# Hybrid encoder layer: two of the output projection's weight chunks split into hi and lo during the in-projection, kept in DRAM, and loaded in the attention

## The chip, the cores and the metric

One NeuronCore of a Trainium2 chip runs the whole program; the other cores are idle. The metric is the device time of one execution in microseconds (us). The kernel before was run three times beside the runs of this study.

## What is computed

One layer of a hybrid encoder in fp32, on 1024 prompt tokens and 256 sample tokens (1280 in all, ten tiles of 128), with model width 1024:

```python
n = _rms_norm(h, g_mix, NORM_EPS)
z = jnp.einsum('bsd,dc->bsc', n, w_in).astype(f32)
qa, ka, va, qb, kb, vb = jnp.split(z, cuts, axis=-1)
oa = _diff_attention(qa, ka, va, lam, _alibi_slopes())
oa = _rms_norm(oa, g_subln, SUBLN_EPS) * (1.0 - lam_init)
ob = _gqa_attention(qb, kb, vb)
mixed = jnp.concatenate([oa, ob], axis=-1).astype(h.dtype)
h = h + jnp.einsum('bsc,cd->bsd', mixed, w_out)
```

Mixer A is differential attention (4 heads, two softmax maps each), mixer B grouped-query attention (8 query heads, 2 key heads, with rotary positions). The output projection multiplies the 1024 columns of `mixed` by `w_out` (1024 x 1024). A squared-ReLU MLP, a gated per-layer input and a last norm follow; the change does not touch them.

## The kernel before, in words

**Precision.** TensorE multiplies fp32r operands. Where fp32 accuracy is wanted, an operand is split into hi (a rounding copy, mostly by ACT) and lo (the difference, by DVE or POOL), and a product is made of three matmuls: hi x hi, hi x lo, lo x hi.

**Stages.** In the in-projection (to about 200 us) units of matmuls (`psb`, `psa`) go through the tokens; `norm_rope` (L296 to L318) norms and rotates a `psb` tile with ACT (`sq`), DVE (`zg`, `rb`, `ro`) and POOL. The results are split and written to DRAM (`qd`, `kd`, `vad`, `vbd`) and loaded again as `qt`, `kt`, `vt` in the attention. In the attention (200 to about 600 us) each unit computes scores (`sc`, PE), exponentials (`p`, ACT), transposes (`tr`, PE), their split (`ph` by ACT, `pl` by DVE) and the products with the values (`av`, PE). Mixed outputs are split into `ml` and written to DRAM as `md`. Beside the attention runs side work on PE: first the rest of the q and k columns (`qk_rest`, L811), then the output projection (`out_proj`, L887) in two passes over four chunks each of 128 rows of `w_out`: (0, 1, 4, 5), then (2, 3, 6, 7).

**Weights of the output projection.** `opw_dma` (L860 to L872) loads a chunk's raw rows as two halves of 128x512 (256 KB each), into the tails of residual tiles (`h_sb`) or into slot Q1 (`wor`). `opw_split` (L874 to L885) makes hi on ACT (L883) and lo on POOL (L884), each 128x512, in tiles `ow`. In the first pass chunk 0's raw rows come early, from `qk_rest` (L840), into Q1; chunks 1 and 4 go to the tails of `h_sb`; chunk 5 goes to Q1 as soon as chunk 0's split has read it. Chunks 2 and 3, for the second pass, are loaded and split while the first pass runs. `load_mt` (L890 to L898) loads a token tile of `mixed` (`mt`, 512 KB) and with it rows of x (`h_sb<-in_x`, 512 KB) to which the result is added.

**Early work.** `early_w1` (L468 to L503) is a side generator of the in-projection: it loads blocks of the MLP's first weights, combines and splits them and writes them to DRAM (`wed`). `along` (L505) steps it between the units of the in-projection, and `drain(early)` finishes it at the end.

**What sets the order.** The program is written as interleaved generators; a framework then fixes each engine's static order by a simulated timeline. Every DMA of interest is issued by SP in one queue; each issue also waits until the eighth DMA before it has landed, so a late transfer holds the issues behind it.

Of the kernel before, what the change touches and what calls it, by code (L numbers as in the profile page):

```python
# [14 lines left out]
F32 = mybir.dt.float32  # L15
F32R = mybir.dt.float32r
# [24 lines left out]
def f(ap):  # L41
    return ap.bitcast(F32)
# [3 lines left out]
def encoder_kernel(ctx: ExitStack, tc: tile.TileContext, x, xT, pT, w_in, w_out, w_ff1, w_ff2, w_gate, w_proj,  # L46
# [3 lines left out]
    LEAD = {4: 2000., 5: 2000., 6: 2000.}  # L50
    PRE = 14000
    Y = (0, 1, 1)
    XA = 1
    QM = 0
    AW = (-7, -6, -5, -4)
# [409 lines left out]
    NEW = 2  # L465
    wed = {(p, i): dp.tile([P, 2, 4, P], F32, name=f"wed{p}_{i}") for p in range(NEW) for i in range(1, 8)}

    def early_w1():  # L468
        for p in range(NEW):
            raws = [slot(f"Q{kh}", [P, 4, 256], F32, "w1e") for kh in range(2)]  # L470
            for kh, raw in enumerate(raws):
                load(raw, w_ff1[kh * 512:kh * 512 + 512, p * 256:(p + 1) * 256].rearrange("(k p) c -> p k c", p=P))
            a11, a12, a21, a22 = (raws[x][:, :, c * P:c * P + P] for c in range(2) for x in range(2))
            yield
            for kh, raw in enumerate(raws):
                for k in range(4):
                    S.activation(raw[:, k], raw[:, k], AF.Copy, scale=gmlp[:, 4 * kh + k:4 * kh + k + 1])
            yield

            def out(i, src):  # L480
                hl = bp.tile([P, 2, 4, P], F32R, tag="xt", name="w1o", bufs=2)
                S.activation(hl[:, 0], src, AF.Copy)
                V.tensor_tensor(hl[:, 1], src, f(hl[:, 0]), op=ALU.subtract)
                dma(wed[p, i], f(hl[:]))

            out(1, a11)
            t = bp.tile([P, 2, 4, P], F32, tag="qkl", name="w1t", bufs=1)
            s3, s2 = t[:, 0], t[:, 1]
            V.tensor_tensor(s3, a11, a21, op=ALU.subtract)
            V.tensor_tensor(s2, a22, s3, op=ALU.subtract)  # L490
            yield
            for i, src in ((6, s2), (7, s3), (2, a12)):
                out(i, src)
                yield
            V.tensor_tensor(s3, a12, s2, op=ALU.subtract)
            V.tensor_tensor(s2, a21, a22, op=ALU.add)
            for i, src in ((5, s2), (4, a22), (3, s3)):
                out(i, src)
                yield

    def along(main, side, skip, every):

# [311 lines left out]
    def qk_rest():  # L814
        w = qk_split(qk_dma(0))
        for n, (h, col, dst, sc) in enumerate(qk_items):
            more = n + 1 < len(qk_items)
            raws = qk_dma(n + 1) if more else None
            wh, wl = w
            for ci, (c0, cn) in enumerate(TCH):  # L820
                ps = pj("psa")
                pr = []
                for k in range(KD):
                    pr += [(wh[k], xh[:, k, c0:c0 + cn]), (wl[k], xh[:, k, c0:c0 + cn]), (wh[k], xl[:, k, c0:c0 + cn])]
                yield from mm_gen(ps[:, :cn], pr, 3)

                def evac(ps=ps, c0=c0, cn=cn, dst=dst, sc=sc, eng=V if LV and not more and ci == 2 else G):
                    hl = zp.tile([P, 2, 512], F32R, tag="zl", name="zl")
                    z = f(hl[:, 1, :cn])
                    V.scalar_tensor_tensor(z, ps[:, :cn], sc, R[:, c0:c0 + cn], op0=ALU.mult, op1=ALU.mult)  # L830
                    S.activation(hl[:, 0, :cn], z, AF.Copy)
                    eng.tensor_tensor(hl[:, 1, :cn], z, f(hl[:, 0, :cn]), op=ALU.subtract)
                    dma(dst[:, :, c0:c0 + cn].rearrange("v p t -> p v t"), f(hl[:, :, :cn]))

                deferred.append(evac)
                yield 0.0
                if ci == 0 and more:
                    w = qk_split(raws)
                elif ci == 0:
                    op_state["w0"] = opw_dma(0, "Q1")  # L840
            qk_done.append(n)

    op_state = {}
# [27 lines left out]
            dma(raws[i], w_out[ch * P:(ch + 1) * P, i * 512:i * 512 + 512])  # L871
        return raws  # L872

    def opw_split(raws):  # L874
        n = next(ow_n) % 5
        if n < 2:
            w = slot(f"H{5 + n}", [P, 2, D], F32R, "ow")
            a, b = w[:, 0], w[:, 1]
        else:
            a, b = (slot(f"W{2 * n - 4 + i}", [P, D], F32R, "ow")[:] for i in range(2))  # L880
        for i, raw in enumerate(raws):
            c = slice(i * 512, i * 512 + 512)
            S.activation(a[:, c], raw, AF.Copy)  # L883
            G.tensor_tensor(b[:, c], raw, f(a[:, c]), op=ALU.subtract)  # L884
        return a, b  # L885

    def out_proj(chs, ws, ahead, banks, first):  # L887
# [10 lines left out]
                        dma(h_row(t_), x[t_ * P:(t_ + 1) * P])  # L898

        if first:  # L900
            raws = [op_state.pop("w0"), opw_dma(chs[1]), opw_dma(chs[2])]
            for n in range(4):
                for _ in range(Y[n > 0]):
                    yield 0.0
                ws.append(opw_split(raws.pop(0)))
                if n == 0:
                    raws.append(opw_dma(chs[3], "Q1"))
                    load_mt(0)
        else:
            raws = []  # L910
# [774 lines left out]
```

## Time and profile before

| | |
|---|---|
| median of 3 runs | 1704.44 us (1703.85 to 1705.3) |
| the profiled execution's own time | 1704.98 us |
| its span, first to last instruction | 1703.2 us |
| granted TensorE clock, mean over the span | 0.997 |
| busy: PE, DVE, ACT, POOL | 98%, 69%, 51%, 39% |
| DMA | 278.28 MB, mean 163 GB/s |

Times in the rows are from the span's start. Busy is the share of a stretch in which the engine executes an instruction; an idle time in square brackets stands before the instruction, with what ended it. The granted clock is 1.00 at 2.4 GHz.

### The profile page before, as it was taken

To read this page: it belongs to the slowest core of one execution; us is meant where nothing else is said; L and a number is where in the kernel's file an instruction comes from. 1 tells how busy PE (TensorE), PEld (TensorE's weight loads), DVE (VectorE), ACT (ScalarE), POOL (GpSimd) and SP (SyncE) were. 2 spreads that over 40 slices of the span, in tenths; PEclk is the share of its full clock that TensorE was granted. 3 is DMA by queue.
4 is the path that set the end of the run, shared out by engine and by line. 5 is a ranking of instruction groups with operands and counts; after the bars stand their busy time and mean duration, and the time that the engine had idled before them with its cause. 6 is when DMAs were issued, how large, how long until landed. Compare 5 with 4: busy or idle time off the path is not lost.

```text
span 1703.2 us, 27269 instructions
## 1 busy us (share of the span) xinstructions
PE 1666.5 (98%) x9849; PEld 1488.6 (87%) x9849; DVE 1177.2 (69%) x2119; ACT 868.3 (51%) x1749; POOL 658.4 (39%) x647
## 2 busy tenths in 40 slices
PE   8999999999899999999999999999999999999997
PEld 8999889888788888889999999998888888888886
DVE  7788588787887878578666666665655865445666
ACT  8543377677766767674333233333433333354644
POOL 1224455555653445424655666520533400001441
PEclk9999999999999999999999999999999999999999
DMA  9767844433953624495343434359666466532111
GB/s 316 228 225 246 233 141 124 138 92 108 269 156 118 165 69 127 134 308 181 132 156 127 138 131 150 122 198 376 202 216 195 130 205 193 169 114 73 35 44 50
DMA packets 191867, 278.28 MB, mean 163 GB/s; under 512 B 13674, under 2 KB 121076, under 8 KB 191732
## 3 DMA queue, kind: packets, MB, share of 16 engines
q1 hardware_dynamic: 189988, 271.28, 49.7%
q0 software_dynamic: 1600, 5.24, 1.0%
q8 instruction: 78, 1.28, 0.3%
q14 instruction: 57, 0.47, 0.1%
q10 hardware_dynamic: 144, 0.00, 0.0%
HBM read 182.63 MB, written 88.61 MB: 159 GB/s over the span
## 4 chain that ended last, share of the span: by engine, by line
PE 79%; DVE 7%; ACT 4%; issue 4%; DMA 3%; POOL 3%; SPq 0%; POOLq 0%; ACTq 0%; DVEq 0%
PE psa L255 6%; PE sc L642 5%; PE psb L255 5%; PE av L720 5%; PE pso L255 4%; PE tr L696 3%; PE psv L255 3%; PE psg L1576 2%; DVE pl L707 1%; DMA h_sb<-in_x 1%; DVE mm L659 1%; PE f__16295 L156 1%; PE f__15255 L156 1%; PE f__16637 L156 1%; PE f__15600 L156 1%
## 5 line engine op out<-in xcount | busy, mean ns | idle before, releaser
L1373 ACT ACTIVATE ao<-ar 128x1280 fp32r<-128x1280 f32 x56 | 71.3, 1275 | 187.5 <-PE f__16299 L156 37.8
L642 PE MATMUL sc<-kt,qt 128*128 128x512 f32 (+1 forms) x576 | 157.0, 392 | 6.9 <-ACT p L667 4.6
L707 DVE TENSOR_TENSOR pl<-tr,ph 128x512 fp32r<-128x512 f32 x204 | 137.9, 684 | 33.5 <-ACT ph L702 32.3
L1375 DVE TENSOR_TENSOR ao<-ar,ao 128x1280 fp32r<-128x1280 f32 x56 | 93.3, 1666 | 94.0 <-ACT ao L1373 94.0
L702 ACT ACTIVATE ph<-tr 128x512 fp32r<-128x512 f32 x204 | 119.8, 595 | 56.9 <-PE tr L696 50.4
L255 PE MATMUL pso<-ow,mt 128*128 128x512 f32 x480 | 119.4, 395 | 4.2 <-ACT ow L883 1.8
L696 PE MATMUL tr<-ident,p 128*128 128x128 f32 x768 | 116.0, 274 | 5.7 <-DVE pl L707 4.9
L642 PEld LDWEIGHTS sc<-kt,qt 128*128 128x128 f32 x576 | 99.4, 190 | 24.8 <-ACT p L667 6.1
L1576 PE MATMUL psg<-gw,n 128*128 128x512 f32 (+1 forms) x504 | 115.4, 384 | 0.0
L696 PEld LDWEIGHTS tr<-ident,p 128*128 128x128 f32 x768 | 91.8, 141 | 22.5 <-DVE pl L707 8.6
L1576 PEld LDWEIGHTS psg<-gw,n 128*128 128x128 f32 x504 | 90.8, 188 | 19.5
L255 PEld LDWEIGHTS pso<-ow,mt 128*128 128x128 f32 x480 | 87.5, 188 | 22.4 <-DVE osq L747 2.0
L1094 POOL TENSOR_SCALAR w1r<-w1r,gmlp 128x256 f32<-128x256 f32 x112 | 79.7, 728 | 67.6 <-DMA w1r<-in_w_ff 67.6
L720 PE MATMUL av<-ph,vt 128*128 128x256 f32 x544 | 102.4, 289 | 1.1 <-ACT ph L702 0.5
L681 POOL TENSOR_SCALAR p<-p,rl 128x1024 f32<-128x1024 f32 x64 | 76.0, 1188 | 51.3 <-DVE rl L679 46.6
L1167 ACT ACTIVATE w<-w1s 128x512 fp32r<-128x512 f32 x56 | 35.2, 628 | 116.5 <-POOL w1s L1174 49.4
L659 DVE TENSOR_REDUCE mm<-sc 128x1 f32<-128x1024 f32 (+1 forms) x80 | 84.2, 1055 | 8.8 <-PE sc L642 8.3
L720 PE MATMUL av<-pl,vt 128*128 128x256 f32 x408 | 89.5, 301 | 0.0
L720 PEld LDWEIGHTS av<-ph,vt 128*128 128x128 f32 x544 | 82.4, 190 | 6.6 <-ACT ph L702 0.9
L667 ACT ACTIVATE p<-sc,mm 128x1024 f32<-128x1024 f32 x64 | 71.3, 1114 | 25.5 <-DVE mm L659 18.5
L655 DVE CUSTOM_DVE_ANT_0 p<-sc,dist 128x1024 f32<-128x1024 f32 x64 | 77.6, 1218 | 7.9 <-PE sc L642 3.8
L664 ACT ACTIVATE p<-p,mm 128x1024 f32<-128x1024 f32 x64 | 73.5, 1149 | 18.0 <-DVE mm L655 17.3
(1520 smaller groups left out, 4717.2 us busy)
## 6 DMA issues: line engine op xcount, KB each, us to landing
ar<-ad SPq DMA_DIRECT2D x56, 640.0 KB, 4.0
w2r<-in_w_ff SPq DMA_DIRECT2D x56, 512.0 KB, 4.6
qt<-qd SPq DMA_DIRECT2D x160, 128.0 KB, 3.1
ad<-q SPq DMA_DIRECT2D x64, 320.0 KB, 3.0
ad<-qs SPq DMA_DIRECT2D x48, 320.0 KB, 2.2
w1r<-in_w_ff SPq DMA_DIRECT2D x28, 512.0 KB, 4.3
md<-ml SPq DMA_DIRECT2D x40, 256.0 KB, 2.5
mt<-md SPq DMA_DIRECT2D x20, 512.0 KB, 5.4
```

The source lines that it names most:

```text
L255: PE.matmul(ps, a, b, start=i == 0, stop=i == n - 1)
L642: PE.matmul(ps[:, h0:h0 + n], shared["q"][:, cc, v, i * P:(i + 1) * P], kt[:, s0 + h0:s0 + h0 + n], start=v == 0, stop=v == 1)
L655: V.tensor_tensor_reduce(out=p[:, :sn], in0=ps[:, :sn], in1=dst_t[:, off:off + sn], scale=SLOPES[idx], scalar=3.0e38, op0=ALU.add, op1=ALU ...
L659: V.tensor_reduce(out=st["m", i][:, 0:1], in_=ps[:, :sn], axis=AX.X, op=ALU.max, negate=True)
L681: G.tensor_scalar(p[:, :sn], p[:, :sn], rl[:, 0:1], 1.0, op0=ALU.mult, op1=ALU.mult)
L696: PE.transpose(t[:, jj, i * P:(i + 1) * P], st["ws"][i][:, j * P:(j + 1) * P], ident)
L702: S.activation(ph, st["tr", j2], AF.Copy)
L707: V.tensor_tensor(pl, st["tr", j2], f(st["ph", j2][:]), op=ALU.subtract)
L720: PE.matmul(st["av"][:, :256], x_, y_, start=j2 == 0 and n == 0, stop=j2 == nj - 1 and n == len(pr) - 1)
L1094: G.tensor_scalar(raw[:, k], raw[:, k], gmlp[:, 4 * kh + k:4 * kh + k + 1], 1.0, op0=ALU.mult, op1=ALU.mult)
L1375: V.tensor_tensor(ao[:, 1], a, f(ao[:, 0]), op=ALU.subtract)
L1576: ends[:] = [PE.matmul(ps, a, b, start=m == 0, stop=m == len(pr) - 1)]
```

## The change

`early_w1` gets a last loop: for chunks 0 and 1 it loads the raw rows of `w_out` (512 KB), splits them in halves with ACT and DVE, and writes hi and lo to new DRAM tiles `wod` (four writes of 512 KB). In the first pass of the output projection `opw_fetch` loads hi and lo of these chunks from there (two DMAs of 512 KB per chunk) into the `ow` tiles; only chunks 4 and 5 are loaded raw and split, both in the tails of `h_sb`. The load from `qk_rest` and Q1's use for chunk 5 go away. `YF` is not used.

```diff
+    OWP = (0, 1)
+    wod = {ch: dp.tile([P, 2, D], F32, name=f"wod{ch}") for ch in OWP}
+
     def early_w1():
...
+        for ch in OWP:
+            raw = bp.tile([P, 2, 512], F32, tag="qkl", name="wo_r", bufs=1)
+            load(raw, w_out[ch * P:(ch + 1) * P, :].rearrange("p (i c) -> p i c", i=2))
+            yield
+            for i in range(2):
+                hl = bp.tile([P, 2, 512], F32R, tag="xt", name="wo_o", bufs=2)
+                S.activation(hl[:, 0], raw[:, i], AF.Copy)
+                V.tensor_tensor(hl[:, 1], raw[:, i], f(hl[:, 0]), op=ALU.subtract)
+                dma(wod[ch][:, :, i * 512:i * 512 + 512], f(hl[:]))
...
                 if ci == 0 and more:
                     w = qk_split(raws)
-                elif ci == 0:
-                    op_state["w0"] = opw_dma(0, "Q1")
...
-    def opw_split(raws):
+    def opw_slot():
         n = next(ow_n) % 5
         if n < 2:
             w = slot(f"H{5 + n}", [P, 2, D], F32R, "ow")
-            a, b = w[:, 0], w[:, 1]
-        else:
-            a, b = (slot(f"W{2 * n - 4 + i}", [P, D], F32R, "ow")[:] for i in range(2))
+            return w[:, 0], w[:, 1]
+        return tuple(slot(f"W{2 * n - 4 + i}", [P, D], F32R, "ow")[:] for i in range(2))
+
+    def opw_fetch(ch):
+
+        ab = opw_slot()
+        for v in range(2):
+            dma(f(ab[v]), wod[ch][:, v])
+        return ab
+
+    def opw_split(raws):
+        a, b = opw_slot()
         for i, raw in enumerate(raws):
...
         if first:
-            raws = [op_state.pop("w0"), opw_dma(chs[1]), opw_dma(chs[2])]
-            for n in range(4):
-                for _ in range(Y[n > 0]):
-                    yield 0.0
-                ws.append(opw_split(raws.pop(0)))
+            raws = [opw_dma(ch) for ch in chs if ch not in OWP]
+            for n, ch in enumerate(chs):
+                if ch in OWP:
+                    ws.append(opw_fetch(ch))
+                else:
+                    yield 0.0
+                    ws.append(opw_split(raws.pop(0)))
                 if n == 0:
-                    raws.append(opw_dma(chs[3], "Q1"))
                     load_mt(0)
```

**In the in-projection, SP's queue after the change**, from the last writes of the MLP's early weights (`wed`) on; `wo_r` is the raw chunk, `wo_o` its split.

```order
L488 DMA wed_3_1301<-w1o 128x1024
L94 DMA wo_r<-in_w_out 128x1024
L583 DMA qt<-qd_64 64x2x256
L337 DMA qd_66<-qkl 128x2x512
L337 DMA qd_67<-qkl 128x2x512
L567 DMA kt<-kd_68 64x1280 x4
L404 DMA qd_60<-zl 128x2x512
L513 DMA wod_1306<-wo_o 256x1x512 x2
L94 DMA wo_r<-in_w_out 128x1024
L404 DMA qd_60<-zl 128x2x512
L513 DMA wod_1307<-wo_o 256x1x512
L811 DMA rawq<-in_w_in 128x4x128
```

On ACT the first pair of copies stands between the square of one `psb` tile and the split of a `psa` tile (`zl`):

```order
L301 ACTIVATE sq<-psb,rstd_95 128x256
L511 ACTIVATE wo_o<-wo_r 128x512 x2
L402 ACTIVATE zl<-zl 128x512
L140 ACTIVATE rq4u<-rq4v 128x4
L141 ACTIVATE rr<-rq4u 128x4
```

All rows with `wo_r` and `wo_o` are new; the rest stands as before, `zl` right behind `sq`. On DVE the subtractions come behind `ro` and ahead of the next `zg`.

**At the start of the output projection, SP's queue before:**

```order
L871 DMA h_sb<-in_w_out 128x512 x4
L894 DMA mt<-md_79 128x8x128
L898 DMA h_sb<-in_x 128x1024 x2
L894 DMA mt<-md_79 128x8x128
L898 DMA h_sb<-in_x 128x1024
L569 DMA qt<-qd_66 64x2x256
L871 DMA wor<-in_w_out 128x512 x2
L569 DMA qt<-qd_66 64x2x256 x2
L559 DMA vt_6352<-vbd_78 128x10x128
L871 DMA h_sb<-in_w_out 128x512 x4
L594 DMA md_79<-ml 128x2x256
```

and now (`ow<-wod` are the fetches; the first four `h_sb<-in_w_out` are chunks 4 and 5, the later four chunks 2 and 3):

```order
L883 DMA h_sb<-in_w_out 128x512 x4
L897 DMA ow<-wod_1306 128x1024 x2
L915 DMA mt<-md_79 128x8x128
L919 DMA h_sb<-in_x 128x1024 x2
L897 DMA ow<-wod_1307 128x1024 x2
L915 DMA mt<-md_79 128x8x128
L919 DMA h_sb<-in_x 128x1024
L583 DMA qt<-qd_66 64x2x256 x2
L573 DMA vt_6369<-vbd_78 128x10x128
L883 DMA h_sb<-in_w_out 128x512 x4
L608 DMA md_79<-ml 128x2x256
```

The fetches stand ahead of the first `mt` and of the raw rows of chunks 2 and 3; `wor` is gone. (In both, one more pair of `mt` and x rows and a further `qt` stand in rows left out here.) PE's order there before, from the first matmuls of the projection (`pso`) on:

```order
L255 MATMUL pso<-ow,mt 128x512 x4
L720 MATMUL av<-ph,vt_3166 128x256 x2
L696 MATMUL tr<-ident,p 128x128 x4
L720 MATMUL av<-pl,vt_3166 128x256 x2
L642 MATMUL sc<-kt,qt 128x512 x4
L255 MATMUL pso<-ow,mt 128x512 x3
L696 MATMUL tr<-ident,p 128x128 x4
```

and now:

```order
L656 MATMUL sc<-kt,qt 128x512 x4
L256 MATMUL pso<-ow,mt 128x512 x3
L710 MATMUL tr<-ident,p 128x128 x8
L656 MATMUL sc<-kt,qt 128x512 x4
L734 MATMUL av<-ph,vt_4918 128x256 x4
```

The first four `pso` no longer stand ahead of `av`; the projection begins where its second group stood.

**ACT at the copies of chunk 5 and chunk 2 before** (`ow<-wor` and the `ow<-h_sb` behind it):

```order
L664 ACTIVATE p,ll<-p,mm 128x1024 x2
L702 ACTIVATE ph<-tr 128x512
L883 ACTIVATE ow<-wor 128x512 x2
L702 ACTIVATE ph<-tr 128x512
L734 ACTIVATE osq<-av 128x256
L735 ACTIVATE o<-av,gsub 128x256
L702 ACTIVATE ph<-tr 128x512
L745 ACTIVATE or<-av,eps_t 128x256
L883 ACTIVATE ow<-h_sb 128x512
L702 ACTIVATE ph<-tr 128x512
L746 ACTIVATE or<-or 128x256
L664 ACTIVATE p,ll<-p,mm 128x1024
```

and now:

```order
L749 ACTIVATE o<-av,gsub 128x256
L716 ACTIVATE ph<-tr 128x512
L759 ACTIVATE or<-av,eps_t 128x256
L716 ACTIVATE ph<-tr 128x512
L760 ACTIVATE or<-or 128x256
L678 ACTIVATE p,ll<-p,mm 128x1024 x2
L904 ACTIVATE ow<-h_sb 128x512
L716 ACTIVATE ph<-tr 128x512
L681 ACTIVATE p,ll<-sc,mm 128x1024
L904 ACTIVATE ow<-h_sb 128x512
```

The copies of `wor` are gone, and chunk 2's first copy has moved behind both exponentials. Up to the start of the output projection the orders of PE, DVE, ACT and POOL differ only by the new copies and subtractions; from there to about 550 us (of the time before) they are dealt anew.

## Rows read from the trace of the kernel before

**Rows 1.** The page, part 1: busy us, share of the span, instructions.

```profile
PE 1666.5 (98%) x9849; PEld 1488.6 (87%) x9849; DVE 1177.2 (69%) x2119; ACT 868.3 (51%) x1749; POOL 658.4 (39%) x647
```

**Rows 2.** Windows: stretch, length; busy us of each engine; granted clock, DMA share, GB/s.

```profile
426.00:468.00 42.00, 37.28 (x227) 32.02 (x226) 33.98 (x58) 31.88 (x64) 28.17 (x27) 0.96 1.01 269
442.00:446.00 4.00, 2.04 (x12) 1.51 (x11) 3.32 (x6) 3.95 (x9) 4.00 (x3) 1.00 1.04 355
458.00:462.00 4.00, 1.81 (x10) 1.15 (x9) 1.43 (x3) 2.62 (x6) 1.97 (x2) 0.98 1.13 236
462.00:466.00 4.00, 4.00 (x14) 3.29 (x14) 3.33 (x6) 1.80 (x5) 0.91 (x2) 0.60 1.02 312
```

**Rows 3.** Waits of PE in 400:560: total us, times, longest us.

```profile
PE sc L642 <- ACT p L667: 2.4, 3, 1.7
...
PE pso L255 <- ACT ow L883: 1.8, 1, 1.8
```

**Rows 4.** Timeline of PE, 440:476: start us, us, instruction, count, idle before.

```profile
446.76 1.07 PE L255 MATMUL pso<-ow,mt 128*128 128x512 f32 x4
...
448.59 1.09 PE L642 MATMUL sc<-kt,qt 128*128 128x512 f32 x4
449.52 0.86 PE L255 MATMUL pso<-ow,mt 128*128 128x512 f32 x3
...
460.00 0.50 PE L255 MATMUL pso<-ow,mt 128*128 128x512 f32 x1 [1.76 <-ACT ow L883]
...
461.36 0.86 PE L255 MATMUL pso<-ow,mt 128*128 128x512 f32 x2 [0.42 <-POOL ow L884]
...
463.58 1.93 PE L642 MATMUL sc<-kt,qt 128*128 128x512 f32 x4
465.35 2.91 PE L255 MATMUL pso<-ow,mt 128*128 128x512 f32 x12
```

**Rows 5.** Timeline of ACT, 438:476.

```profile
440.14 1.16 ACT L883 ACTIVATE ow<-wor 128x512 fp32r<-128x512 f32 x2
441.73 0.63 ACT L883 ACTIVATE ow<-h_sb 128x512 fp32r<-128x512 f32 x1 [0.43 <-DMA h_sb<-in_w_out]
...
459.32 1.32 ACT L883 ACTIVATE ow<-wor 128x512 fp32r<-128x512 f32 x2 [3.06 <-DMA wor<-in_w_out]
...
464.93 0.63 ACT L883 ACTIVATE ow<-h_sb 128x512 fp32r<-128x512 f32 x1 [1.34 <-DMA h_sb<-in_w_out]
...
467.90 1.14 ACT L664 ACTIVATE p<-p,mm 128x1024 f32<-128x1024 f32 x1
```

**Rows 6.** Timeline of SP's DMA queue, 436:476.

```profile
439.51 0.56 SPq L894 DMA_DIRECT2D mt<-md  x1
```

**Rows 7.** Windows, in-projection.

```profile
175.00:185.00 10.00, 10.00 (x73) 9.29 (x72) 8.22 (x18) 4.63 (x11) 6.26 (x7) 1.00 0.34 116
```

**Rows 8.** Timeline of SP's DMA queue, 150:186.

```profile
162.97 0.54 SPq L484 DMA_DIRECT2D wed<-w1o  x1
```

**Rows 9.** DMA issues in 155:175: count, KB each, median us to landing.

```profile
wed<-w1o SPq DMA_DIRECT2D x3, 512.0 KB, 4.6
kt<-kd SPq DMA_DIRECT2D x4, 320.0 KB, 6.7
...
qd<-zl SPq DMA_DIRECT2D x1, 512.0 KB, 7.9
```

**Rows 10.** Timeline of ACT, 160:186.

```profile
163.80 0.47 ACT L300 ACTIVATE sq<-psb,rstd 128x256 f32<-128x256 f32 x1 [0.82 <-PE psb L255]
166.29 0.63 ACT L401 ACTIVATE zl<-zl 128x512 fp32r<-128x512 f32 x1 [2.02 <-DVE zl L400]
```

**Rows 11.** Timeline of DVE, 160:186.

```profile
161.33 0.69 DVE L483 TENSOR_TENSOR w1o<-w1t,w1o 128x512 fp32r<-128x512 f32 x1 [0.94 <-ACT w1o L482]
...
170.14 0.48 DVE L301 SCALAR_TENSOR_TENSOR zg<-psb,rstd,gq 128x256 f32<-128x256 f32 x1 [0.45 <-ACT sq L300]
```

**Rows 12.** Timeline of PE, 174:180.

```profile
176.09 0.36 PE L255 MATMUL psb<-whp,xh 128*128 128x256 f32 x1
```

More of the change, by code (lines that the diff above doesn't have):

```diff
@@ L52, in encoder_kernel @@
     Y = (0, 1, 1)
+    YF = 2
     XA = 1
```

## The prediction

> **What bounds the kernel now.** I read the page's busy shares first, then the windows around the start of the output projection, then the waits and the engines' timelines there, and last the DMA lists and the in-projection.
>
> TensorE (PE) is busy 98% of the span [rows 1], so only what makes PE idle or slow counts. The windows show one such place: in 458:462 PE is busy for 1.81 of 4 us, and in 462:466 it is busy throughout at a granted clock of 0.60 [rows 2]. The waits name the cause: a matmul of the output projection (`pso`) waits 1.8 us for ScalarE's (ACT's) hi copy of w_out, line 883 [rows 3]. In the timelines, ACT stood 3.06 us in front of the copies of chunk 5 (`wor`) because their data had not landed [rows 5]; PE then stood 1.76 us for ACT and 0.42 us for GpSimd's (POOL's) lo [rows 4]. 1.76 + 0.42 = 2.18 us is all the idle time of 458:462 (4 - 1.81 = 2.19). Slow matmuls follow: four `sc` take 1.93 us at 463.58 against 1.09 at 448.59 [rows 4]. Behind all of it is the DMA queue, whose share is 1.01 at 269 GB/s through 426:468 [rows 2].
>
> **What the change takes away.** Chunk 5 is no longer loaded into Q1 in the middle of this stretch: its raw rows come with the first loads, and chunks 0 and 1 are not split here. So the stall above goes:
> - PE's idle time, 1.76 + 0.42 = 2.2 us;
> - the half clock behind it: 4 us at 0.60 lose 4 x 0.40 = 1.6 us [rows 2]. The two levels are 1.2 and 2.4 GHz, and 0.60 is a mean over both.
>
> Together **-3.8 us**. Of four chunk splits, two leave ACT and POOL here. ACT's pair of copies at 440.14 only filled a wait: ACT stood again, 0.43 us, for the first raw half at 441.73 [rows 5], and that load keeps its place at the head of SyncE's (SP's) queue. So PE's 1.7 us behind the exponential (`sc<-ACT p` [rows 3], of which the windows show 442:446 with PE at 2.04 of 4) stays, and I cost that part at nothing.
>
> **What it adds in the attention.** SP now issues four fetches of 512 KB (2.1 MB) and no `wor` load there (0.52 MB less): 1.57 MB more before the first raw half of chunk 2. The queue is full, so this is time for whatever stands behind. I price it by the rows: at 355 GB/s (442:446) 4.4 us, at 269 (426:468) 5.8, at 236 (458:462) 6.7 [rows 2]. I take 355, because 442:446 moves mostly x rows of 128x1024, the shape of a fetch.
>
> First new wait: `mt` for the first token tile was issued at 439.51 [rows 6] and was there at the latest at 446.76, when PE began `pso` without waiting [rows 4]. Now two fetches, 1.05 MB, stand ahead of it: 3.0 us at 355, so it lands by 449.7 or before. PE's order has lost four `pso` matmuls ahead of that place, so PE comes there 0.93 us before the 449.52 where the second `pso` group stood, at about 448.6. The wait is 0 to 1.1 us at this rate, 2.1 at 269, 2.6 at 236. 446.76 is an upper bound of the old landing, so I take **+0.9**.
>
> Second new wait: ACT's copy of chunk 2's first half. Before, ACT stood 1.34 us for that load, which ended at 464.93 [rows 5], and that hid under slow matmuls. Now the load ends 4.4 us later, 469.3. ACT comes to the copy after both exponentials of the round: before, the second of them ended at 467.90 + 1.14 = 469.0 [rows 5]; less the 3.8 us that PE no longer loses and less one copy of 0.63, that is 464.6. So ACT is held 4.7 us, longer than the hold that goes. What is queued behind it: a `ph` copy, and PE's transposes and `av` wait for that one. Cover: the old hold of 3.06 cost PE 2.2, so 0.9 was covered by matmuls already released; and PE now has in front of the dependent ones twelve `pso` of the next tile, 2.91 us by the row at 465.35 [rows 4]. Where the scheduler put them, I count some 3.2 us of cover out of these 3.8. The price is 4.7 - 3.2 = **+1.5**. The bounds are 0 (the load lands early) and, at 269 GB/s with only the twelve as cover, 6.1 - 2.9 = 3.2. After the second wait PE has lost 2.4 us in two pieces, each below the 1.76 that came before the slow stretch, and I count no fall of the clock.
>
> **What it adds in the in-projection.** Each chunk is loaded (512 KB), copied by ACT (2 x 0.63, as `ow<-h_sb` [rows 5]), subtracted by VectorE (DVE, 2 x 0.69 us, by the like subtraction of w1 at 161.33 [rows 11]) and written (2 x 512 KB). PE is busy in all of 175:185, and the DMA share there is 0.34 [rows 7], so the writes, and the second chunk's load, find room. Only the first chunk is tight. SP issues its load behind the last `wed` write (162.97 + 0.54, so 163.5) [rows 8]. The loads and writes about it took 4.6 (`wed`), 6.7 (`kt`) and 7.9 us (`qd<-zl`) to land [rows 9]; I take 5.7, which gives 169.2, with 168.1 and 171.4 as the ends. ACT is held from `sq` (163.80 + 0.47) until then, with the `zl` copy that was at 166.29 behind it [rows 10]; its two copies, `zl` and the small steps of the norm end some 2.1 us after the landing, DVE's chain to `ro` takes 2 more, its two subtractions 1.4, and then comes `zg`, which was at 170.14 [rows 11]: 169.2 + 5.5 = 174.7, and 0.5 for itself. It frees the psum buffer that PE fills at 176.09 [rows 12]. So it fits by 0.9 us: **0**, and at 171.4 the price is +1.3. The second pair on DVE pushes a `zg` by 1.4 us whose buffer is filled a whole unit of PE's work later: nothing. SP's `wod` writes wait for DVE; behind them stands `rawq`, and SP had time there.
>
> **The sum.** -3.8 + 0.9 + 1.5 + 0 = **-1.4 us**. The profiled execution's own time was 1704.98 us, 0.54 above the median, which is within the spread of the runs; taken off the median, 1704.4 - 1.4 = **1703.0 us**. The order of the instructions behind this place, to about 550 us, is dealt anew as well; the waits there are of some 1 us each, and I allow +-1 for them.
>
> **Rivals.**
> 1. No new waits: the fetches are early enough, and neither `mt` nor chunk 2 is waited for. For it: `mt` may have landed well before 446.76, and ACT's 464.6 may be too early. Against it: a DMA share of 1.01 leaves no room [rows 2]. -3.8: 1700.6 us.
> 2. The queue runs slow, and this becomes slower than before. Place: `mt` and the raw rows of chunk 2. At 236 GB/s, which 458:462 showed, `mt` costs 2.6, ACT's hold is 464.93 + 6.7 - 464.6 = 7.0, less 2.9 of cover 4.1, and such a wait is followed by the half clock, 1.6: 8.3 - 3.8 = +4.5, 1708.9 us. It decides just under 269 GB/s, where 2.1 + 3.2 + 1.6 - 3.8 = +3.1. For it: the mean of the stretch is just that. Against it: the fetches have long rows, and `mt`'s wait also moves ACT, so the two don't add in full.
> 3. The clock falls again. In this trace 442:446 has almost the same idle time (1.96 us) as 458:462 (2.19), and only the second is followed by slow matmuls [rows 2, 4]; a new idle time of 2.4 us lies beyond both. The forecast and 1.6: +0.2, 1704.6 us. The Trainium skill ("TensorE: Matmul & The Clock Gate", Part 1) says that the throttled clock is the default, and only activity releases it; by that rule any shift of an idle time carries its slow stretch along. The trace agrees for the idle time of 458:462 and not for that of 442:446.
> 4. The in-projection holds PE after all: a landing at 171.4, +1.3, 1704.3 us.
>
> **How the numbers follow.** The forecast has 0.40, rival 1 0.21, rival 2 0.16, rival 3 0.18, rival 4 0.05. A measurement of this kernel can tell 0.2%, 3.4 us, from no change: faster means under 1701.0, slower over 1707.9. Rival 1 is faster, and a little of the forecast with its +-1 and a cover that is longer: 0.22. Rival 2 is slower: 0.16. The rest is the same: 0.62. The range goes from rival 1 with 0.7 of the later order off, 1699.9, to just short of rival 2 in full, 1708.2.
>
> **What would show it.** Right: no `pso` wait for line 883's old copies at 460, clock 1.00 where 462:466 was 0.60; a `pso` wait of about 1 us for `mt` near 449; ACT idle 4 to 5 us before a copy `ow<-h_sb` that ends about 469, with PE idle near 470; and no PE idle time in 165:185. Wrong: PE idle in all of 168:182 beyond 1 us, an unbroken PE from 446 to 480 (rival 1), over 4 us of PE idle time between 448 and 474 (rival 2), or a clock under 0.9 in any window after 448 (rival 3).

## The result: slower by 0.4%, in the in-projection and in the attention

The changed kernel took 1711.86 us, the median of four runs (1709.76 to 1714.41); the kernel before took 1704.87 beside it (four runs, 1703.85 to 1705.64). The ratio is 1.0040, with a 95% interval of 1.0029 to 1.0052. The forecast was 1703.0 with a range up to 1708.2. The profiled execution of the changed kernel is the fastest of its four, 1709.76 us with a span of 1708.0.

The page of the changed kernel, part 1, against [rows 1]:

```profile
PE 1666.7 (98%) x9849; PEld 1489.9 (87%) x9849; DVE 1177.7 (69%) x2123; ACT 867.2 (51%) x1749; POOL 655.1 (38%) x643
```

TensorE (PE) is busy for the same time as before, and the span has grown by 4.8 us: PE's idle time has grown. Within a stretch the granted clock counts as well, since slow matmuls count as busy. Four of the changed kernel's idle places, in PE's timeline:

```profile
185.01 0.44 PE L342 MATMUL trb<-ident,ro 128*128 128x128 f32 x2 [1.10 <-DVE ro L319]
...
447.26 1.92 PE L656 MATMUL sc<-kt,qt 128*128 128x512 f32 x4 [2.21 <-ACT p L681]
...
498.56 2.42 PE L656 MATMUL sc<-kt,qt 128*128 128x512 f32 x6 [2.15 <-DVE mm L669]
...
697.67 0.70 PE L753 MATMUL av<-osq,mean_m 128*128 128x256 f32 x2 [1.58 <-ACT o L749]
```

The `pso` stall for chunk 5's copies [rows 3, 4] isn't among them. The windows of the changed kernel (stretch, length, busy us of each engine, granted clock, DMA share, GB/s) answer to [rows 2]:

```profile
444.00:448.00 4.00, 1.79 (x12) 1.48 (x11) 3.30 (x6) 3.31 (x7) 4.00 (x4) 0.93 0.89 328
448.00:452.00 4.00, 4.00 (x20) 3.53 (x20) 2.41 (x4) 3.24 (x8) 4.00 (x4) 0.64 1.09 373
452.00:472.00 20.00, 20.00 (x125) 17.59 (x124) 14.56 (x27) 12.00 (x24) 7.89 (x10) 1.00 1.11 292
...
496.00:500.00 4.00, 1.85 (x8) 1.32 (x7) 3.93 (x6) 2.19 (x5) 0.04 (x1) 0.83 0.39 116
500.00:504.00 4.00, 4.00 (x18) 3.49 (x17) 3.09 (x8) 2.53 (x6) 3.08 (x5) 0.74 0.00 0
432.00:480.00 48.00, 44.70 (x278) 39.12 (x277) 38.35 (x68) 33.76 (x68) 31.15 (x33) 0.96 1.07 286
480.00:560.00 80.00, 75.22 (x459) 65.22 (x458) 63.30 (x121) 53.03 (x110) 32.02 (x36) 0.98 0.47 142
```

The last two stretches of the kernel before:

```profile
432.00:480.00 48.00, 43.18 (x261) 36.97 (x260) 38.46 (x66) 34.82 (x71) 33.82 (x33) 0.96 1.03 276
480.00:560.00 80.00, 76.68 (x470) 66.07 (x469) 64.03 (x123) 53.90 (x111) 32.97 (x38) 1.00 0.42 127
```

From 452 to 472, where before the stall stood, PE is now unbroken at full clock. But the clock of 432:480 is 0.96 in both: the slow stretch stands at 448:452 now, behind the wait for the exponential. PE gained 1.5 us in 432:480 (44.70 - 43.18) and lost as much in 480:560 (1.46), where in addition 0.02 of the clock is missing (0.02 x 75 = 1.5 us). These windows lie at fixed times, though, and the changed kernel came into them 2.2 us late, so the next measure is the safer one.

To place the rest, I compare the start of the same PE or ACT instruction in both profiles and follow how far the changed kernel lags. The lag grows by 1.0 us up to 152 us, +1.3 through the in-projection (152 to 235), -0.1 to 432, +0.2 to 549, +0.6 to 720, +1.7 to 774. The first of these is not the change's: up to 72 us both kernels run the same instructions, and over the 13 profiles after the first that part came out between -1.8 and +2.2 us. Whether the last is the change's stays open. There ACT waits for loads (`nlo`, `hd`); of the kernels named below, in_only, inplace, inplace_in_only, ml2, inplace_ml2 and inplace_y2 lost 1.5 to 3.0 us there, in_only and inplace_in_only with the order of instructions of the kernel before, and the other six -0.3 to +0.4, among them after_again, which is the changed kernel itself.

### The profile page after: what moved, and what is told of

Its sections match the earlier page's. It is cut to its first block, busy times and chain, and to the rows that moved or that the text cites. A ratio compares the mean times of both kernels' runs of the same rounds, so it can differ in the third digit from the quotient of the medians.

```text
span 1708.0 us, 27276 instructions
## 1 busy us (share of the span) xinstructions
PE 1666.7 (98%) x9849; PEld 1489.9 (87%) x9849; DVE 1177.7 (69%) x2123; ACT 867.2 (51%) x1749; POOL 655.1 (38%) x643
## 4 chain that ended last, share of the span: by engine, by line
PE 75%; DVE 8%; DMA 6%; ACT 5%; issue 4%; POOL 2%; SPq 0%; POOLq 0%; DVEq 0%; ACTq 0%
PE sc L656 6%; PE av L734 5%; PE psa L256 5%; PE pso L256 4%; PE tr L710 4%; PE psb L256 2%; PE psv L256 2%; PE psg L1598 2%; DMA xt<-in_x 1%; DMA xr<-in_xT 1%; PE f__15267 L157 1%; PE f__16307 L157 1%; PE f__16649 L157 1%; DVE nlo L1223 1%; PE f__15612 L157 1%
```

## The experiments

Twelve more runs were made, each beside the kernel before on its own chip (1705.35, 1704.78, 1704.88 and 1705.32 us, medians of 12 to 23 runs). The results first; the last two columns are PE's busy us and granted clock in 432:480 and 480:560 of the profiled execution.

```
kernel            median us  runs  ratio to before (95%)      432:480      480:560
before                                                        43.18 0.96   76.68 1.00
changed           1711.86     4    1.0040 (1.0029-1.0052)     44.70 0.96   75.22 0.98
after_again       1710.68     5    1.0036 (1.0022-1.0049)     44.84 0.96   73.92 1.00
in_only           1708.78    11    1.0022 (1.0013-1.0031)     42.87 1.00   76.46 1.00
att_only          1707.95    11    1.0018 (1.0009-1.0027)     44.79 0.96   75.50 0.98
early_load        1710.37     5    1.0032 (1.0019-1.0044)     45.05 0.96   74.48 0.98
inplace           1710.02     5    1.0032 (1.0020-1.0045)     42.62 1.00   73.10 0.98
inplace_in_only   1706.07    11    1.0007 (0.9998-1.0016)     44.41 0.96   76.81 1.00
ml2               1710.64     5    1.0036 (1.0022-1.0050)     45.16 0.96   76.24 1.00
inplace_ml2       1708.78    10    1.0024 (1.0014-1.0033)     44.28 0.96   76.46 0.98
before_b          1703.88     1                               44.29 0.96   76.61 1.00
five              1705.41    12    1.0005 (0.9996-1.0014)     44.22 1.00   76.01 1.00
traffic           1705.44    11    1.0002 (0.9994-1.0011)     44.26 0.96   77.58 1.00
inplace_y2        1709.15     8    1.0022 (1.0011-1.0032)     44.69 0.96   73.49 0.98
```

The profiled executions of att_only and traffic were the fastest of their eleven, and that of inplace_y2 the slowest of its eight, so a single profile need not show what the median does.

### The change cut in two

**after_again** is the changed kernel once more. **in_only** is the kernel before with the new loop of `early_w1` alone; nothing reads what it writes. **att_only** is the changed attention alone, without that loop; its fetches read tiles of `wed`, so its projection is computed with other numbers.

```diff
in_only, against the kernel before
+        for ch in OWP:
+            raw = bp.tile([P, 2, 512], F32, tag="qkl", name="wo_r", bufs=1)
...
+                dma(wod[ch][:, :, i * 512:i * 512 + 512], f(hl[:]))
att_only, against the changed kernel
-        for ch in OWP:
-            raw = bp.tile([P, 2, 512], F32, tag="qkl", name="wo_r", bufs=1)
...
-            dma(f(ab[v]), wod[ch][:, v])
+            dma(f(ab[v]), wed[0, (1, 6, 7, 2)[2 * ch + v]].rearrange("p a k c -> p (a k c)"))
```

> The changed kernel once more, for a second trace and more times. In its first trace it lies 4.7 us behind the kernel before, and the lag builds up at four places: 0.9 us by 72 us (in code that both share), 1.3 us at 164 to 181 (in-projection), 0.2 us net from 443 to 549 (output projection), 2.3 us at 640 to 760 (last attention rounds and norms). Theory 1, the work added to the in-projection and the order dealt anew behind it cost the time: the lags at 164 to 181 (1.0 to 1.5) and in 440 to 560 (-1 to +3) are there again, the first is not (below 0.3), and the median is 1710 to 1713. Theory 2, the new DRAM tiles shift what lies in DRAM and make the loads slower everywhere: the lag of 0.9 by 72 us is there again.

> The kernel before with the added work in the in-projection alone: the two chunks are loaded, split and written to DRAM, and nothing reads them; the attention is that of before, in the same order on all engines. Theory 1: the hold of ACT behind the first chunk's load costs 1.0 to 1.5 us and nothing else does, 1705.9 to 1706.4. Theory 2: that and the 0.9 at the start, 1706.8 to 1707.3. Rival, the hold is made up later in the attention: 1704.9, no change.

> The changed kernel without the added work in the in-projection: the four fetches of 512 KB read other tiles of the same size from DRAM (the early weights of the MLP), so that the output projection multiplies by the wrong numbers; the order from there on is that of the changed kernel. Theory 1: the removed stall is given back by new ones within 440 to 560, net 0 to +3 there, and the lag at 640 to 760 is there if it comes from the order: 1705 to 1710. Rival, the in-projection is the whole cost and the attention gains what was forecast: 1701 to 1703.5.

Measured: in_only +3.4 us against its before (1708.78 - 1705.35), att_only +2.6; together 6.0, where the whole change gave 7.0 and, again, 5.3. Both halves cost, and they add. in_only came out above all that I had expected of it (1707.3 at most). after_again lagged by 1.6 us at 72 us, where I had expected less than 0.3; in_only, which has the same new DRAM tiles, was 1.6 us ahead there, so the tiles don't set that part.

in_only shows where its half goes. Its ACT, and then its PE:

```profile
168.73 1.15 ACT L510 ACTIVATE wo_o<-wo_r 128x512 fp32r<-128x512 f32 x2 [6.10 <-DMA wo_r<-in_w_out]
```

```profile
183.59 0.44 PE L341 MATMUL trb<-ident,ro 128*128 128x128 f32 x2 [2.13 <-DVE ro L318]
```

ACT is held for the raw chunk, as I had counted, and no psum buffer holds PE. But the norm chain that runs through ACT and DVE ends late, in `ro`, and PE's next work is the transposes of `ro`. In the changed kernel DVE writes that `ro` at 184.53; before, at 181.56, ready 0.8 us ahead of the transposes at 182.80. DVE's timeline, of the changed kernel and of the kernel before:

```profile
184.53 0.42 DVE L319 TENSOR_TENSOR ro<-ra,rr 128x256 f32<-128x256 f32 x1
184.88 1.29 DVE L512 TENSOR_TENSOR wo_o<-wo_r,wo_o 128x512 fp32r<-128x512 f32 x2
```

```profile
181.56 0.42 DVE L318 TENSOR_TENSOR ro<-ra,rr 128x256 f32<-128x256 f32 x1
```

The stall of PE at that place: 1.10 us in the changed kernel, 2.13 in in_only, 2.18 in after_again, whose ACT was held for 6.00 us. In the lag, the in-projection cost 1.3, 3.0 and 4.6 us. The 4.6 hold a slow stretch as well: behind after_again's stall the clock was 0.57 over 4 us, which loses 0.43 x 4.00 = 1.7 us, and in the other two it was 1.00. The window of after_again:

```profile
188.00:192.00 4.00, 4.00 (x12) 3.11 (x11) 4.00 (x9) 1.55 (x5) 2.81 (x4) 0.57 0.71 214
```

att_only has the changed kernel's 480:560 without that, 75.50 us at 0.98 in the table, and these two of its stalls in PE's timeline. But in the lag this profile, the fastest of its runs, lost nothing from 432 to 549 (-0.5 us) and is only 0.3 us behind the first profile of the kernel before at 774. So att_only's +2.6 stands in its median, and its own profile doesn't show where it lies.

```profile
445.20 2.07 PE L645 MATMUL sc<-kt,qt 128*128 128x512 f32 x4 [2.62 <-ACT p L670]
...
495.29 2.01 PE L645 MATMUL sc<-kt,qt 128*128 128x512 f32 x6 [2.15 <-DVE mm L658]
```

### The in-projection: when the raw rows come, and what ACT waits for

**early_load** loads both raw chunks into Q0 and Q1 before the last step of `early_w1`'s own loop. **inplace** does that too, and writes lo over the raw rows, so that a chunk needs one `xt` buffer where it needed two. **inplace_in_only** is the kernel before with inplace's in-projection alone.

```diff
early_load, against the changed kernel
+                if p == NEW - 1 and i == 4:
+                    for ch in OWP:
+                        wor[ch] = slot(f"Q{ch}", [P, 2, 512], F32, "wor")
+                        load(wor[ch], w_out[ch * P:(ch + 1) * P, :].rearrange("p (i c) -> p i c", i=2))
inplace, beside that
+            hi = bp.tile([P, 2, 512], F32R, tag="xt", name="wo_o", bufs=2)
             for i in range(2):
...
+                S.activation(hi[:, i], f(raw[:, i]), AF.Copy)
+                V.tensor_tensor(raw[:, i], f(raw[:, i]), f(hi[:, i]), op=ALU.subtract)
```

> The changed kernel with the raw rows of both chunks loaded earlier, into the two slots that the MLP's early weights leave, so that ACT does not wait for them; the order from the output projection on is the same. Theory 1: the lag at 164 to 181 goes, PE has no idle time there, and the time falls by 1.0 to 1.5 us against the changed kernel run beside it. Rival, ACT's copies and DVE's subtractions themselves hold the in-projection, not the load: the lag stays at 1 us or more.

> The changed kernel with the in-projection's split in another form: both chunks' raw rows are loaded some 6 us earlier, into the slots Q0 and Q1, and lo is written over them, so that a chunk needs one of the two buffers that the early weights' writes hold and not two. ACT's four copies and DVE's four subtractions stay where they were, PE's and POOL's orders are those of the changed kernel. Theory 1, ACT's wait (for the load, or for a buffer that a write still holds) delays the chain of norm steps, and that chain holds PE at the transposes near 185 us: ACT waits under 1 us there, the lag of 160 to 222 us falls from 1.3, 4.6 and 2.2 in the runs so far to below 0.7, and the time to some 2 us above what the attention alone showed... 1707.5 to 1708.5. Rival, the 2.6 us of subtractions on DVE delay the chain by themselves: the lag stays at 1.5 or more and the time at 1710 to 1711.

> The kernel before with this other form of the in-projection's split alone, nothing reads the result; all orders of the attention are those of before. Theory 1: 1705.3 to 1706.0, no change against before, where the first form cost 3.4 us. Rival (DVE's subtractions): 1707.5 to 1709.

early_load gained nothing (1710.37): ACT no longer waited for the raw rows, but for the buffers of its results, which hold until earlier writes have gone out. Its ACT, and then its PE:

```profile
169.35 0.63 ACT L515 ACTIVATE wo_o<-wor 128x512 fp32r<-128x512 f32 x1 [3.49 <-DMA wed<-w1o]
...
176.81 0.63 ACT L515 ACTIVATE wo_o<-wor 128x512 fp32r<-128x512 f32 x1 [1.67 <-DMA wod<-wo_o]
```

```profile
185.13 0.44 PE L342 MATMUL trb<-ident,ro 128*128 128x128 f32 x2 [1.95 <-DVE ro L319]
```

With both waits gone, PE's stall shrinks to a quarter. inplace:

```profile
183.08 0.44 PE L342 MATMUL trb<-ident,ro 128*128 128x128 f32 x2 [0.52 <-DVE ro L319]
```

inplace_in_only has no such stall; in the lag its in-projection costs nothing (0.0 us against in_only's 3.0), and its ratio, 1.0007, can't be told from 1. So most of in_only's 3.4 us is ACT's hold, and not the copies, the subtractions or the bytes written, which are the same in both. But inplace as a whole stays at +5.2 us (1710.02 - 1704.78), where I had expected 1708.5 at most: what it loses lies mostly behind the in-projection.

### The attention: the prize, the traffic, and the order

**before_b** is the kernel before, in a second execution. **five** is the kernel before with chunk 5 alone split in the in-projection (in inplace's way) and fetched. **traffic** is the kernel before with three copies of 512 KB from DRAM to DRAM behind the first raw loads, the traffic that the change adds.

```diff
five, against the kernel before
-            for n in range(4):
+            for n in range(3):
...
-                    raws.append(opw_dma(chs[3], "Q1"))
...
+            ws.append(opw_fetch(chs[3]))
traffic, against the kernel before
+            pads = [dp.tile([P, D], F32, name=f"pad{i}") for i in range(3)]
+            with tc.issue_after(lastd[0].ins):
+                for i in range(3):
+                    dma(pads[i][:, :], w_out[i * P:(i + 1) * P, :])
```

> The kernel before once more, for a second trace. In its first trace PE stood 2.2 us for the copies of chunk 5 and then ran at half clock; in two runs that have its order in the attention (the in-projection changed alone, in two forms) PE stood 1.7 and 0.2 us there and no half clock followed. Theory 1: the price of this stall differs from execution to execution, and 3.8 us is its upper end: here it is between 0.2 and 2.2 us, with a half clock in one case of two at most. Rival: it is 3.5 to 4 us in the kernel before, and the in-projection's added work moved it in the other two.

> The kernel before with chunk 5 alone, the one whose raw rows came late, split in the in-projection (in the form that does not wait: raw rows early, lo over them) and fetched as hi and lo behind the first mt and its x rows; chunk 0 is preloaded, chunks 1 and 4 are loaded and split as before. 0.5 MB more than before go through the queue there, not 1.6. Theory 1, the extra traffic and the order dealt anew are what gives the gain back: PE's wait for line 883 at 460 is gone, no wait over 1.5 us is new between 440 and 560, and the time is 1702.5 to 1704.5, 0 to 2 us under before. Rival, any new order loses as much as the stall was worth: 1705 to 1708.

> The kernel before with three copies of 512 KB from DRAM to DRAM (rows of w_out to tiles that nothing reads) put behind the first four raw loads of the output projection, 1.6 MB as in the changed kernel; no work is moved. Theory 1, the traffic ahead of mt and of the raw chunks costs time by itself, through the order that it makes the scheduler deal and through waits: 1707 to 1712. Rival, the queue hides it: 1704 to 1706.

before_b shows that the stall the change was to remove is not there in every execution of the kernel before. Its windows over the stretches of [rows 2] and, ahead of them, over 444:452; then PE's one long wait there:

```profile
444.00:448.00 4.00, 2.40 (x11) 2.15 (x12) 2.99 (x7) 3.98 (x8) 4.00 (x4) 0.86 1.07 375
448.00:452.00 4.00, 4.00 (x18) 3.42 (x17) 1.61 (x5) 3.03 (x7) 4.00 (x5) 0.71 1.13 334
458.00:462.00 4.00, 3.99 (x23) 2.91 (x21) 3.58 (x5) 3.13 (x7) 3.75 (x3) 1.00 1.14 252
462.00:466.00 4.00, 3.37 (x16) 2.48 (x16) 4.00 (x8) 2.98 (x7) 2.14 (x2) 1.00 1.07 329
```

```profile
445.60 1.19 PE L642 MATMUL sc<-kt,qt 128*128 128x512 f32 x4 [2.45 <-ACT p L667]
```

458:462 is full, and the half clock stands at 444:452, behind the exponential, as it does in the changed kernel. The same instructions in the same order lost 1.76 + 0.42 us for chunk 5 in the profile I read, 1.27 + 0.42 in in_only (with no slow stretch), and none in inplace_in_only and here. So the 3.8 us were one execution's. Nor would all of them have been won: in before_b and inplace_in_only PE stood longer for the exponential instead (2.45 and 2.36 us, against 1.66 in the first profile), the slow stretch came behind that wait, and the stretch from 432 to 549 was only 1.2 and 1.5 us shorter in the lag.

five removes that stall, and gains nothing that can be told (1.0005, so between 0.7 us less and 2.4 us more), where I had expected up to 2 us. This agrees with a small prize, but doesn't measure it alone: five adds a chunk's work to the in-projection and has a new order in the attention, and its rival, that a new order loses what the stall was worth, isn't ruled out. traffic costs nothing either (1.0002), with its queue as full as the changed kernel's (share 1.07, 306 GB/s in 432:480). So the fetches' bytes alone aren't the cost; traffic has raw loads of its own, though, and no engine waits for its copies. In both kernels the orders of the four engines were dealt anew as well, so a new order by itself need not cost.

What is left is the changed order, and what the engines wait for in it. PE is busy for 73.10 to 75.50 us of 480:560 in the changed kernel, after_again, att_only, early_load, inplace and inplace_y2, against 76.01 to 77.58 in the six whose attention is the old one, or the old one but for chunk 5 or the added copies. In the changed order with `ml` doubled, below, it is 76.24 and 76.46. The lag from 432 to 549, against the first profile, is +0.2, +0.6, -0.5, +0.6 and +3.9 us in the first five, whose order there is one and the same, and -1.2, -0.3 and -1.5 in before_b, in_only and inplace_in_only, whose order is that of before. The means are +0.96 and, with the first profile as 0, -0.75 us: 1.7 us apart; 549 to 720 adds 0.5. That is near att_only's +2.6, but one order alone spreads over 4.4 us, so it is an estimate.

The stall that all kernels with the changed order share is that of 498, of 2.15 us in each; only inplace_y2 lacks it. DVE's timeline of the changed kernel shows what stands ahead of the maximum that PE waits for:

```profile
496.07 1.28 DVE L691 SCALAR_TENSOR_TENSOR p<-p,rl 128x1024 f32<-128x1024 f32 x1 [0.38 <-POOL p L689]
497.28 1.22 DVE L669 CUSTOM_DVE_ANT_0 p<-sc,dist 128x1024 f32<-128x1024 f32 x1
```

The combine of another head's `p`, itself held for POOL, comes first on DVE, and then the maximum; PE has nothing else in its order between. In the order before, the like wait was 0.63 + 0.48 us (PE's timeline):

```profile
495.18 0.66 PE L696 MATMUL tr<-ident,p 128*128 128x128 f32 x4 [0.63 <-DVE pl L707]
496.32 1.20 PE L642 MATMUL sc<-kt,qt 128*128 128x512 f32 x4 [0.48 <-DVE mm L655]
```

**ml2** is the changed kernel with two `ml` buffers, since ACT waited there for one (2.39 us at 486.61, until the write of `md` had landed); **inplace_ml2** is inplace with the same edit. **inplace_y2** is inplace with one more step of the attention's order ahead of each raw chunk's split, so that the same work is dealt once more.

```diff
ml2, against the changed kernel
-        "o": ([P, 256], F32, 3), "or": ([P, 256], F32, 1), "ml": ([P, 2, 256], F32R, 1),
+        "o": ([P, 256], F32, 3), "or": ([P, 256], F32, 1), "ml": ([P, 2, 256], F32R, 2),
inplace_y2, against inplace
                     yield 0.0
+                    yield 0.0
                     ws.append(opw_split(raws.pop(0)))
```

> The changed kernel with two buffers in place of one for ml, the split of a mixed output on its way to DRAM; PE's order in the attention is the same. In the changed kernel ACT stands 2.4 and 1.1 us at 484 to 490 until the write of the ml before has landed, because 1.6 MB more stand in the queue; DVE then runs late, and PE stands 2.2 us at 498 for a maximum, with the half clock behind. Theory 1, this wait makes the stall: both go, and the time falls by 2 to 4 us, to 1707 to 1709. Rival, the stall at 498 comes from the order in which DVE's work was dealt: ACT's waits go, PE's stall at 498 stays above 1.5 us, and the time falls by less than 1.

> Both together. If both theories hold, the gains add: 1703 to 1706, about the time of the kernel before or 1 to 2 us under it. If neither, 1710 to 1711.

> The kernel inplace (1710.02, cheap in-projection, the change's attention) with one more step of the attention's order between the first two splits of raw chunks: same work, same traffic, but the four engines' orders from about 452 to 550 us are dealt anew once more. Theory 1, what is left of the loss lies in how the order was dealt (the 2.15 us stall of sc for DVE's maximum at 498 and the half clock behind it): that stall is gone or at another place, the stretch from 432 to 549 is 2 to 4 us shorter than in inplace, and the median comes to 1706 to 1708. Rival, it lies in the fetches and their traffic whatever the order: the stretch stays at inplace's length, and the median at 1709 to 1711. The stall behind the exponential at 444 to 448 stays by both.

ml2 made 484:496 whole, 12.00 us of PE where the changed kernel has 10.67, and left the stall at 498 as it was, so `ml` is not that stall's cause. The windows of ml2, and its PE:

```profile
484.00:496.00 12.00, 12.00 (x81) 10.65 (x79) 9.72 (x19) 9.68 (x20) 4.12 (x4) 1.00 0.72 235
...
496.00:500.00 4.00, 1.78 (x8) 0.97 (x6) 4.00 (x7) 2.77 (x6) 0.00 (x0) 1.00 0.47 131
```

```profile
498.29 1.64 PE L656 MATMUL sc<-kt,qt 128*128 128x512 f32 x6 [2.15 <-DVE mm L669]
```

Yet the stretch from 432 to 549 came to -2.8 us in the lag, and to -1.1 in inplace_ml2, with PE's order that of the changed kernel and only a few `ml` copies moved on ACT and their partners on POOL. So what is lost there isn't in PE's order alone: ACT's wait for the write of `md` has a large part in it. Over the five kernels with one order the stretch grows with that wait: 2.10 us in att_only (-0.5), 2.39 in the changed kernel (+0.2), 3.12 in early_load (+0.6), 3.35 in after_again (+0.6) and 4.38 in inplace (+3.9). In the old order it was 1.25 to 1.81. ACT's timeline of the kernel before, the changed kernel and inplace:

```profile
480.32 0.42 ACT L589 ACTIVATE ml<-o 128x256 fp32r<-128x256 f32 x1 [1.37 <-DMA md<-ml]
```

```profile
486.61 0.42 ACT L603 ACTIVATE ml<-o 128x256 fp32r<-128x256 f32 x1 [2.39 <-DMA md<-ml]
```

```profile
488.27 0.42 ACT L609 ACTIVATE ml<-o 128x256 fp32r<-128x256 f32 x1 [4.38 <-DMA md<-ml]
```

In the whole time this didn't pay. ml2 gave back 3.9 us behind 549 (inplace_ml2 3.8), 3.0 of them between 720 and 774, with ACT held 5.30 us for a load of the next stage among the places; its 1710.64 is no better than after_again. ACT's timeline of ml2:

```profile
737.55 1.15 ACT L1036 ACTIVATE h_sb<-h_sb,nst 128x1024 f32<-128x1024 f32 x1 [5.30 <-DMA hd<-h_sb]
```

inplace_ml2 stays at +4.0, where inplace had +5.2, with intervals that overlap.

inplace_y2's 432:480 is as good as the changed kernel's, and the wait for the maximum at 498 is gone. Other waits stand in its place, in PE's timeline:

```profile
497.48 0.66 PE L716 MATMUL tr<-ident,p 128*128 128x128 f32 x4 [0.85 <-DVE pl L727]
499.49 3.05 PE L256 MATMUL pso<-ow,mt 128*128 128x512 f32 x12 [1.35 <-DVE osq L767]
...
538.71 1.74 PE L662 MATMUL sc<-kt,qt 128*128 128x512 f32 x4 [1.84 <-ACT p L687]
```

480:560 is no better (73.49 at 0.98, in the slowest of its runs), ACT's wait for the write of `md` is 5.21 us, and the stretch from 432 to 560 came to +3.2 us in the lag; the median is at +3.8 where inplace had +5.2, with intervals that overlap. The half of the expectation that the stall would move came true; that the time would come down didn't. So the 2.15 us stall isn't what decides this stretch: inplace_y2 loses there without it, and ml2 and inplace_ml2 lose nothing there with it. No kernel tried beat the kernel before.

## Why the prediction was wrong

**"-3.8" for the stall and its half clock: the step that failed first.** The stall did go, as forecast, and 452:472 is whole. But its price came from one execution. In before_b none of it was there, the stretch was 1.2 us shorter for that and not 3.8, and five, which takes it away, gained nothing that can be told. The half clock did not go at all: it moved to 448:452, behind the exponential's wait, which I had said "stays" and cost at nothing. That was rival 3 (+1.6), from a stall of the old order and not from the new wait that I had in mind. The Trainium skill ("TensorE: Matmul & The Clock Gate", Part 1) says that the throttled clock is the default and that activity releases it; rival 3 took from this that an idle time carries its slow stretch along. The runs agree with that for 448:452 and 496:504 of the changed kernel and not for ml2, whose same 2.15 us stall at 498 was followed by a clock of 1.00.

**"+0.9" for `mt` and "+1.5" for chunk 2: the landings right, the prices too high.** The copy of chunk 2's first half stands in ACT's timeline at

```profile
471.00 0.63 ACT L904 ACTIVATE ow<-h_sb 128x512 fp32r<-128x512 f32 x1 [3.34 <-DMA h_sb<-in_w_out]
```

6.1 us later than before, of which 2.2 was the lag that the kernel brought into this stretch: 3.9 against the 4.4 that I had worked out. ACT was held 3.34 us where I said 4.7, and PE lost 0.5 us behind it (a `sc` that waited for `pq`), where I said 1.5: the cover was longer. `mt` was issued at 442.65 and landed 8.7 us later, at 451.35, or 449.2 without the lag, where I had 449.7 at the latest. It cost nothing in the changed kernel, because PE, behind the exponential's wait and the slow stretch, came to its first `pso` only at 452.40; in inplace PE waited for it for 1.38 us. The rate of 355 GB/s was taken for the rows of x, which by the size of the packets (4096 B) were 0.58 of the 1.42 MB that moved in 442:446, and not most of it. In this one profile PE gained 1.5 us in 432:480, next to my -1.4; that is luck, since the terms were others.

**"0" for the in-projection: failed.** The hold of ACT was within what I had worked out: 4.41 us, to 170.14, where I had 169.2 with 171.4 as the end.

```profile
170.14 1.15 ACT L511 ACTIVATE wo_o<-wo_r 128x512 fp32r<-128x512 f32 x2 [4.41 <-DMA wo_r<-in_w_out]
```

I followed it to one thing that PE needs, the psum buffer behind `zg`, found 0.9 us of room there, and stopped. The same chain ends in `ro`, and PE's transposes wait for that: 1.10 to 2.18 us. Rival 4 had the event (+1.3, the number of the first profile) by the wrong place and with a chance of 0.05 (only in after_again did PE stand for `zg` there, 0.30 us); in_only's median says +3.4, and with the hold gone (inplace_in_only) nothing that can be told is left.

**"+-1" for the order dealt anew: too small.** The new order has a 2.15 us stall where 0.48 and 0.63 were, the slow stretch behind it (0.17 x 1.85 + 0.26 x 4.00 = 1.4 us), a longer wait of ACT for the write of `md` (2.10 to 4.38 us, against 1.25 to 1.81), and at 697 a stall of 1.58 us where the order before has 0.73, in a swap that lies behind the 550 us to which I had seen the orders differ (+0.5 to +0.6 in the lag of 549 to 720, in five profiles with the changed attention). By the means over the profiles that is some 1.7 + 0.5 = 2.2 us, above my margin.

Put together, in medians: in-projection +3.4, attention +2.6. The in-projection's cause is shown: with ACT's hold the stall at `ro` comes, and without it the cost goes. The attention's is shown in part: the prize is small, ACT's wait for `md`'s write lengthens 432 to 549, and how the +2.6 divides between that wait, the stall at 498 with the clock behind it and the 0.6 us near 697 stays open; so does the 720 to 774 of ml2 and others. Single profiles differ by +-2 us in shared code, so they don't separate it. Rival 2, the one I gave for slower, had the wrong place: the queue was as full as it feared, but PE hardly stood for `mt` and the raw rows, while ACT stood for a write that no rival named.

## What to carry to other kernels

Before a stall is priced, read a second execution of the same kernel: a wait for a transfer can be 2 us in one and nothing in the next, with another wait in its place. When an engine is held, follow its whole chain to each thing that the bounding engine takes from it, data as well as buffers. And where an edit makes a scheduler deal the order anew over 100 us, the new order is a term of its own, to be read engine by engine in the listing of instructions, with its waits for buffers, and not a margin.

## What was not expected of the hardware

The same instructions of the first 70 us took from 1.8 us less to 2.2 us more than in the first profile. With one order of instructions (kernel before, before_b, in_only), the stretch at half clock followed the idle time of 458:462 (before), or the one behind the exponential (before_b), or neither (in_only: 1.00 in all of 432:480, with its stall of 1.27 us in place). Copies of 1.6 MB more in a queue with a DMA share of 1.03 cost nothing that could be told (traffic, 1.0002).
